# The first norm of a transformer layer on one core: block 1's row of scales read from PSUM, block 2's squares elsewhere, block 3's x turned

## The chip, the cores and the metric

The kernel runs on one core of a Trainium2 chip. Its engines work side by side, each through its own instructions in order: TensorE (PE; weight loads are shown as PEld), VectorE (DVE), ScalarE (ACT), GpSimd (POOL), and SyncE (SP), which here issues the DMAs. TensorE writes to PSUM alone; the other operands lie in SBUF. The metric is the time of one execution on the device, in microseconds (us); lower is better.

## The reference

One layer (DEPTH = 1, so the stick-breaking mixer) on 2048 tokens of 1024 features, 16 heads, followed by a SwiGLU FFN of width 2816. Cut to what matters:

```python
sh_m, sc_m, gt_m, sh_f, sc_f, gt_f = split(silu(c) @ ada_w + ada_b, 6)
h = rms_norm(x, norm_g[0]) * (1 + sc_m) + sh_m       # the first norm: the change is here
q, k, v = split(h @ w_qkv, 3)
z = q @ k.T * HEAD_DIM ** -0.5                       # per head, blocks of 128 rows
sp = where(s < t, softplus(z), 0)
a = exp(where(s < t, z - reverse_cumsum(sp), -inf))
x = x + gt_m * rms_norm((a @ v) @ w_o, norm_g[1])
h = rms_norm(x, norm_g[2]) * (1 + sc_f) + sh_f
g, u = split(h @ ffn_w_in, 2)
x = x + gt_f * rms_norm((silu(g) * u) @ ffn_w_out, norm_g[3])

rms_norm(x, g) = x * rsqrt(mean(x * x, -1) + 1e-6) * g
```

## The kernel before, in words

The 2048 tokens are four blocks of 512 (b = 0 to 3); the 1024 features are eight chunks of 128 (k = 0 to 7). The projections want h with features on the partitions, 128 x 512 for each block and chunk, and in two parts: a high part, which is h rounded to TensorE's fp32r type, and a low part, the rest. A product is then three matmuls (mm3, L174 to L176): high by high, high by low, low by high.

The first norm makes these parts (first_norm, L409, with modulate, L378). A block can get its transposed x in two ways. Blocks 0 and 2 load x by rows: the rows are squared and summed on ACT (rms_scale, L165), scaled by their rstd on DVE (L330, L338), turned on TensorE into PSUM (x_turn, L361), and then ACT multiplies by the gain and adds the shift (L383), and DVE rounds (L384) and subtracts (L385). Blocks 1 and 3, named in BY_FEATURES, load x a second time, by columns (cols_load, L313, the kernel argument xt). Of the rows only the rstd is used: spread over 128 columns (L340), it is turned on TensorE into a row of scales that is the same on all partitions (x_share, L352), and ACT copies it to SBUF (L354). scale_cols then multiplies a column chunk by gain and row on DVE (L372) or, for odd k of block 3, by the row alone on GpSimd (L376). modulate finishes: for even k and for all of block 1, ACT adds the shift and rounds (L389), DVE adds and subtracts (L390); for odd k of block 3, ACT applies gain and shift (L394), copies to the high part (L395) and GpSimd subtracts (L397). scale_cols runs up to two chunks ahead of modulate.

The program writes out the order of each engine's instructions by hand: what is traced first runs first on TensorE, ACT, DVE and GpSimd; SP's DMAs are placed by the framework. Buffers have tags with a number of slots; a new tile waits until a slot of its tag is free. Here matter "kt" (7: key tiles, columns of x), "v" (7: value tiles, rows of x), "wraw" (2: raw weights, junk of squares, the parked key and query tiles), "aT" (4: turned attention weights, and early on two weight tiles), "tmp" (4), and the PSUM pools zps (3 banks: scores), tps (2: turned weights) and accps (3: projections, turned values, the attention's sums, turned x).

project computes keys (t = 1), queries (t = 0), values (t = 2) of a pair of heads p and a block b, one mm3 per slice. While it runs for block b, the norm of the next block nb is made beside it: rows are squared and scaled at t = 0 (nb = 2) or t = 1 (nb = 3); chunks 0 to 2 of the norm at slices 2, 4, 6 of t = 2; chunks 3 to 7 at slices 0 to 4 of t = 1 in the next step, three products ahead of their use. Block 1's chunks 4 to 7 are made at the first slices of its own keys.

Attention runs at the same time, in slots of one 128 x 512 tile of scores. In a slot (ORDER_IN_SLOT) come, in order, the sum with values (L672), the scores (L593), one or two slices of the projections with what is beside them, the turning of weights (L644, every second slot), the two sigmoids on ACT (L610, L612), the scan on DVE (L622, L627) with a product on GpSimd (L634), and the turned weights' high part on ACT (L654) and low part on DVE (L660); in odd slots this last pair comes ahead of the sigmoids.

Of the kernel before, what the change touches and what calls it, by code (L numbers as in the profile page):

```python
# [16 lines left out]
P = 128  # L17
# [52 lines left out]

H2_STEP = 3

BY_FEATURES = (1, 3)

NORM_AT = [(2, 2), (2, 4), (2, 6)]

# [26 lines left out]
def hybrid_trunk_kernel(  # L103
# [206 lines left out]
    def cols_load(b, *which):  # L310
        for m in which or range(KC // 2):
            cols = att.tile([P, 2, BT], F32, name=f"xc{b}_{m}", tag="kt", bufs=BUFS["kt"])
            nc.sync.dma_start(cols, xt[b // 2, :, 2 * m : 2 * m + 2])  # L313
            x_cols[b, 2 * m], x_cols[b, 2 * m + 1] = cols[:, 0], cols[:, 1]

    def x_square(b, i):
        if b > 0:
            tok = x_tiles[b, i]
            if b in BY_FEATURES:
                junk = tok  # L320
            else:
                junk = att.tile([P, D], F32, name=f"xj{b}_{i}", tag="wraw", bufs=BUFS["wraw"])
            x_rstd[b, i] = rms_scale(att, tok, f"n0_{b}_{i}", junk=junk)
            return
        xn = att.tile([P, D], F32, name=f"xn{b}_{i}", tag="kt", bufs=BUFS["kt"])
        x_norm[b, i] = xn
        x_rstd[b, i] = rms_scale(att, x_tiles[b, i], f"n0_{b}_{i}", junk=xn)
# [16 lines left out]
    def x_share(b):  # L344

        if b not in BY_FEATURES:
            return
        pool, tag = (tps, "t") if b < 2 else (accps, "acc")
        pt = pool.tile([P, BT], F32, name=f"xr{b}", tag=tag)
        for i in range(4):  # L350
            tok = x_tiles.pop((b, i))
            nc.tensor.transpose(pt[:, i * P : (i + 1) * P], tok[:, :P], ident)  # L352
        x_row[b] = tok[:, BT:]
        nc.scalar.copy(x_row[b], pt)  # L354

    def x_turn(b, k):

# [8 lines left out]
    def scale_cols(b, k):  # L366

        if b not in BY_FEATURES:
            return
        u = x_cols[b, k]  # L370
        if k % 2 == 0 or b == 1:
            nc.vector.scalar_tensor_tensor(  # L372
                u, u, g_eff[:, 0, k : k + 1], x_row[b], op0=ALU.mult, op1=ALU.mult
            )
        else:
            nc.gpsimd.tensor_tensor(u, u, x_row[b], op=ALU.mult)  # L376

    def modulate(hl, b, k):  # L378

        gain, add = g_eff[:, 0, k : k + 1], mod[:, 0, k : k + 1]  # L380
        if b not in BY_FEATURES:
            u = att.tile([P, BT], F32, name=f"hf{b}_{k}", tag="tmp", bufs=BUFS["tmp"])
            nc.scalar.activation(u, x_turn(b, k), AF.Identity, bias=add, scale=gain)  # L383
            nc.vector.tensor_copy(hl[:, 0], u)  # L384
            nc.vector.tensor_tensor(hl[:, 1], u, f32(hl[:, 0]), op=ALU.subtract)  # L385
            return
        u = x_cols.pop((b, k))
        if k % 2 == 0 or b == 1:
            nc.scalar.activation(hl[:, 0], u, AF.Identity, bias=add)  # L389
            nc.vector.scalar_tensor_tensor(  # L390
                hl[:, 1], u, add, f32(hl[:, 0]), op0=ALU.add, op1=ALU.subtract
            )
        else:
            nc.scalar.activation(u, u, AF.Identity, bias=add, scale=gain)  # L394
            nc.scalar.copy(hl[:, 0], u)  # L395
            eng = nc.gpsimd if b == NB - 1 else nc.vector
            eng.tensor_tensor(hl[:, 1], u, f32(hl[:, 0]), op=ALU.subtract)  # L397

    def h_load(p, b):
        h = []  # L400
# [45 lines left out]
    def project(at):  # L446

        p, b = STEPS[at]
        begun = at < 2
        early, parked = (p, b) in EARLY, (p, b) == PARKED  # L450

        nb = STEPS[at + 1][1] if at + 1 < len(STEPS) and STEPS[at + 1][0] == 0 else None
        if STEPS[at] == (PARKED[0], 1):
            unpark()
        h = norm_h[b] if p == 0 or parked else h_load(p, b)

        def product(t):
            if begun:
                if at == 0 and t != 2:
                    first_norm(1, 2 + (t == 0))  # L460
                return first_acc[p, t]
            w = weights[p, t]
            acc = accps.tile([P, BT], F32, name=f"pj{p}_{b}_{t}", tag="acc")
            ahead = b == NB - 1 and p + 1 < NPAIR
            for k in range(KC):
                if t == 1:
                    if p == 0:
                        first_norm(b, k + (4 if b == 1 else 3))
                    if k == 0 and nb == 3:
                        cols_load(3)  # L470
                    if k in (3, 5) and waiting:
                        waiting.pop(0)()
                if nb == 2 and (t, k) == (0, 0):
                    x_load(3)
                square_at = {2: 0, 3: 1}.get(nb)
                if t == square_at and k < 4:
                    x_square(nb, k)
                if t == square_at and 2 <= k < 6:
                    x_spread(nb, k - 2)
                if nb and (t, k) == (0, 1):  # L480
                    x_share(nb)
                if (t, k) in NORM_AT:
                    first_norm(nb, NORM_AT.index((t, k)))
                if ahead and k == 0:
                    load_weights(p + 1, t)
                if ahead and k == 6:
                    split_weights(p + 1, t)
                mm3(acc, (w[0][:, k], w[1][:, k]), (h[k][:, 0], h[k][:, 1]), k == 0, k == KC - 1)
                yield
            return acc  # L490

        def split(acc, tag):
            place = "wraw" if parked else "qkn"
            hl = att.tile([P, 2, BT], F32R, name=f"{tag}n{p}_{b}", tag=place, bufs=BUFS[place])
            nc.scalar.copy(hl[:, 0], acc)
            nc.vector.tensor_tensor(hl[:, 1], acc, f32(hl[:, 0]), op=ALU.subtract)
            return hl

        closing = (p, b) == (NPAIR - 1, NB - 1)
        if closing:  # L500
            wo_load(0, 0, "whl")
            wo_load(0, 1, "ht")
        n = split((yield from product(1)), "k")
        if closing:
            wo_load(0, 2, "whl")
        if parked:
            nc.sync.dma_start(k_park, f32(n))
        else:
            kt = att.tile([P, 2, BT], F32R, name=f"kt{p}_{b}", tag="kt", bufs=BUFS["kt"])
            for e in range(2):  # L510
                for part in range(2):
                    nc.sync.dma_start(
                        f32(kt[part * HD : (part + 1) * HD, e]), f32(n[e * HD : (e + 1) * HD, part])
                    )
            keys[p, b] = kt

        n = split((yield from product(0)), "q")
        if closing:
            wo_load(0, 3, "whl")
        if parked:  # L520
            nc.sync.dma_start(q_park, f32(n))
            for out_of in held:
                nc.sync.dma_start(*out_of)
        else:
            qt = att.tile([P, 2, 2, BT], F32R, name=f"qt{p}_{b}", tag="qt", bufs=BUFS["qt"])
            for e in range(2):
                for half in range(2):
                    nc.sync.dma_start(
                        f32(qt[half * HD : (half + 1) * HD, e]), f32(n[e * HD : (e + 1) * HD])
                    )  # L530
            queries[p, b] = qt
        acc = yield from product(2)
        tag = "w" if early else "tmp"
        vT = att.tile([P, BT], F32, name=f"vT{p}_{b}", tag=tag, bufs=BUFS[tag])
        nc.scalar.copy(vT, acc)

        def values_turn():
            pool, ptag = (zps, "z") if early else (accps, "acc")
            pt = pool.tile([P, 4, 2, HD], F32, name=f"vt{p}_{b}", tag=ptag)
            for i in range(4):  # L540
                nc.tensor.transpose(
                    pt[:, i].rearrange("p e d -> p (e d)"), vT[:, i * P : (i + 1) * P], ident
                )
            v = att.tile([P, 4, 2, 2, HD], F32R, name=f"v{p}_{b}", tag="v", bufs=BUFS["v"])
            nc.scalar.copy(v[:, :, :, 0], pt)
            nc.vector.tensor_tensor(v[:, :, :, 1], pt, f32(v[:, :, :, 0]), op=ALU.subtract)
            if parked:
                nc.sync.dma_start(v_park, f32(v))
            else:
                values[p, b] = v  # L550

        if early:
            waiting.append(values_turn)
            return
        for _ in range(VGAP):
            yield
        values_turn()
# [1200 lines left out]
```

## Time and profile before

| what | us |
|---|---|
| three runs: median (lowest to highest) | 2848.71 (2847.3 to 2853.94) |
| the profiled execution | 2845.32 |
| its span, first to last instruction | 2843.2 |
| TensorE busy in the span | 2800.4 (98%) |
| VectorE busy | 2021.7 (71%) |
| ScalarE busy | 1634.1 (57%) |
| GpSimd busy | 1282.5 (45%) |
| mean granted TensorE clock | 0.997 |

A row of the timeline reads: start in us, length in us, engine, line of the kernel, operation, out<-in by the program's names, shapes, how many were merged, and in brackets the idle time of the engine just before and what ended it. A row of a group (by line) ends in busy us and the mean ns of one; a row asked by tile or line gives the shortest, the median and the longest in ns, and the first and last start in us. A row of the waits gives the total in us, the number of times and the longest. A DMA row gives the KB of one and the us from issue to landing. Starts are counted from the start of the span.

### The profile page before, as it was taken

The page shows a single profiled execution, that of the slowest core. Times are in us where ns is not written, and L with a number is a line of the kernel's source. Part 1 is how long each engine was busy: PE and PEld are TensorE (multiplying, and loading weights), DVE is VectorE, ACT ScalarE, POOL GpSimd, SP SyncE. Part 2 cuts the span into 40 slices and gives each one's busy share as a digit, 9 for nine tenths or more (in the row PEclk, how much of TensorE's full clock was granted, in tenths as well). Part 3 has the DMA queues.
Part 4 walks back from the last instruction along what each step waited for, and adds up shares of the span by engine and source line. Part 5 has one row for each costly group of instructions (what it writes and reads, how often), then busy time and mean ns, then how long its engine had stood idle before and what let it go on. Part 6 is the DMA issues. An engine that isn't in the chain of part 4 may idle for free.

```text
span 2843.2 us, 41829 instructions
## 1 busy us (share of the span) xinstructions
PE 2800.4 (98%) x13853; PEld 2338.5 (82%) x13853; DVE 2021.7 (71%) x2822; ACT 1634.1 (57%) x3274; POOL 1282.5 (45%) x2032
## 2 busy tenths in 40 slices
PE   9899999999999999999999999999999999999998
PEld 7788888888888888887888788888788888888887
DVE  6788888888888888888866766555775655134377
ACT  5787778787777877778645533333433333322243
POOL 0565666676576655666410122222222222544454
PEclk9999999999999999999999999999999999999999
DMA  9774556666665635546389644334453335545575
GB/s 368 285 230 157 186 170 212 211 188 216 196 217 177 218 116 175 193 136 228 97 293 317 196 139 153 120 103 160 127 176 110 112 105 166 191 138 153 181 227 187
DMA packets 239787, 521.05 MB, mean 183 GB/s; under 512 B 22481, under 2 KB 108497, under 8 KB 222674
## 3 DMA queue, kind: packets, MB, share of 16 engines
q1 hardware_dynamic: 239570, 518.38, 56.4%
q8 instruction: 109, 1.79, 0.3%
q14 instruction: 108, 0.88, 0.1%
HBM read 351.04 MB, written 118.49 MB: 165 GB/s over the span
## 4 chain that ended last, share of the span: by engine, by line
PE 84%; DVE 5%; DMA 5%; ACT 2%; issue 2%; POOL 1%; SPq 0%; DVEq 0%; POOLq 0%; ACTq 0%
PE s L174 9%; PE s L175 9%; PE s L176 9%; PE z L593 8%; PE o L672 8%; PE t L644 8%; PE pj L174 5%; PE pj L176 5%; PE pj L175 5%; PE o L176 4%; PE o L174 4%; PE o L175 4%; DMA h_s<-ht 1%; PE y L176 1%; PE y L174 1%
## 5 line engine op out<-in xcount | busy, mean ns | idle before, releaser
L634 POOL TENSOR_TENSOR a<-a,w 128x512 f32<-128x512 f32 (+3 forms) x640 | 621.6, 971 | 217.2 <-DVE w L627 130.3
L627 DVE TENSOR_TENSOR_SCAN w<-z,c,begin 128x512 f32<-128x512 f32 x384 | 489.3, 1278 | 83.9 <-ACT z L612 60.6
L174 PE MATMUL s<-r,l 128*128 128x512 f32 x1232 | 482.3, 391 | 5.1 <-DVE p L1490 3.9
L176 PE MATMUL s<-r,l 128*128 128x512 f32 x1232 | 480.2, 390 | 0.0
L175 PE MATMUL s<-r,l 128*128 128x512 f32 x1232 | 479.9, 390 | 0.0
L610 ACT ACTIVATE a<-z 128x512 f32<-128x512 f32 (+3 forms) x640 | 347.1, 542 | 170.4 <-PE z L593 137.6
L672 PE MATMUL o<-aT,v 128*128 128x512 f32 (+3 forms) x1280 | 385.0, 382 | 0.1
L660 DVE TENSOR_TENSOR aT<-t,aT 128x512 fp32r<-128x512 f32 (+3 forms) x640 | 358.6, 594 | 23.9 <-ACT aT L654 23.4
L593 PE MATMUL z<-kt,qt 128*128 128x512 f32 (+3 forms) x1280 | 363.7, 365 | 0.0
L654 ACT CAST aT<-t 128x512 fp32r<-128x512 f32 (+3 forms) x640 | 313.9, 533 | 73.5 <-PE t L644 63.4
L612 ACT ACTIVATE z<-z 128x512 f32<-128x512 f32 (+3 forms) x640 | 344.8, 539 | 0.0
L1498 POOL TENSOR_TENSOR one<-p,p 128x512 f32<-128x512 f32 x44 | 70.9, 1612 | 579.1 <-issue 322.2
L174 PE MATMUL pj<-ht,w 128*128 128x512 f32 x768 | 308.4, 402 | 4.3 <-issue 1.4
L644 PE MATMUL t<-begin,a 128*128 128x128 f32 x2176 | 295.7, 274 | 13.8 <-DVE aT L660 12.5
L644 PEld LDWEIGHTS t<-begin,a 128*128 128x128 f32 x2176 | 255.7, 141 | 64.1 <-DVE aT L660 14.0
L175 PE MATMUL pj<-ht,w 128*128 128x512 f32 x768 | 301.5, 393 | 2.0 <-DVE ht L390 1.5
L176 PE MATMUL pj<-ht,w 128*128 128x512 f32 x768 | 301.9, 393 | 0.0
L174 PEld LDWEIGHTS s<-r,l 128*128 128x128 f32 x1232 | 231.7, 188 | 56.0 <-ACT l L1351 2.9
L176 PEld LDWEIGHTS s<-r,l 128*128 128x128 f32 x1232 | 231.5, 188 | 48.3
L175 PEld LDWEIGHTS s<-r,l 128*128 128x128 f32 x1232 | 231.7, 188 | 48.0 <-issue 0.5
L622 DVE TENSOR_TENSOR_SCAN w<-z,begin 128x128 f32<-128x128 f32 (+3 forms) x256 | 208.6, 817 | 76.7 <-ACT z L612 67.5
L593 PEld LDWEIGHTS z<-kt,qt 128*128 128x128 f32 x1280 | 231.0, 189 | 37.6 <-DVE w L622 0.2
(178 smaller groups left out, 4879.3 us busy)
## 6 DMA issues: line engine op xcount, KB each, us to landing
ht<-h_s SPq DMA_DIRECT2D x108, 1024.0 KB, 8.2
wi<-in_win SPq DMA_DIRECT2D x86, 512.0 KB, 4.0
qt<-qn SPq DMA_DIRECT2D x124, 256.0 KB, 4.8
ol_qt<-act_s SPq DMA_DIRECT2D x56, 512.0 KB, 3.7
act_s<-S SPq DMA_DIRECT2D x66, 256.0 KB, 4.1
br<-in_wout SPq DMA_DIRECT2D x66, 256.0 KB, 3.5
h_s<-ht SPq DMA_DIRECT2D x16, 1024.0 KB, 9.8
o_s<-os SPq DMA_DIRECT2D x128, 128.0 KB, 2.6
```

Of the source, the lines that this page charges most:

```text
L174: nc.tensor.matmul(acc, lhs[0], rhs[0], start=first, stop=False, **kw)
L175: nc.tensor.matmul(acc, lhs[0], rhs[1], start=False, stop=False, **kw)
L176: nc.tensor.matmul(acc, lhs[1], rhs[0], start=False, stop=last, **kw)
L593: nc.tensor.matmul(z[:, :n], q[:, e, part, r * P : (r + 1) * P], k[:, e, :n], start=part == 0, stop=part == 1,)
L610: nc.scalar.activation(a[:, :n], z[:, :n], AF.Sigmoid, scale=QK_SCALE)
L612: nc.scalar.activation(z[:, :n], z[:, :n], AF.Sigmoid, scale=-QK_SCALE)
L627: nc.vector.tensor_tensor_scan(rest[:, rev], left[:, rev], begin[:, :BT][:, rev], initial=carries[r], op0=ALU.mult, op1=ALU.bypass,)
L634: nc.gpsimd.tensor_tensor(a[:, :n], a[:, :n], rest[:, 1 : n + 1], op=ALU.mult)
L644: nc.tensor.transpose(pt[:, rb * P : (rb + 1) * P], weighed[i, rb][:, j * P : (j + 1) * P], ident)
L654: nc.scalar.copy(hl[:, 0, t0:], pt[:, t0:])
L660: nc.vector.tensor_tensor(hl[:, 1, t0:], pt[:, t0:], f32(hl[:, 0, t0:]), op=ALU.subtract)
L672: nc.tensor.matmul(acc[:, t0:], lhs, hl[:, part, t0:], start=sc == qb and j == 0 and part == 0, stop=sc == 0 and j == 3 and part == 1,)
```

## The change

Block 1 stays by columns. Its row of scales is no longer copied to SBUF: DVE reads it from the PSUM bank in each of the eight chunks. For k = 3, 5 and 7 ACT adds the shift in place, copies to the high part, and GpSimd makes the low part. Block 2's squares write their junk to "aT" instead of "wraw". Block 3 leaves BY_FEATURES: it no longer loads columns, scales its whole rows on DVE, has its x turned on TensorE into an accps bank, and DVE applies gain and shift straight from PSUM to a "tmp" tile; ACT copies that to the high part and GpSimd subtracts, for all eight chunks. Its junk of squares goes to "wraw". The argument xt now holds block 1 alone.

```diff
-BY_FEATURES = (1, 3)
+BY_FEATURES = (1,)
+
+ON_GPSIMD = (3, 5, 7)
...
-            nc.sync.dma_start(cols, xt[b // 2, :, 2 * m : 2 * m + 2])
+            nc.sync.dma_start(cols, xt[:, 2 * m : 2 * m + 2])
...
-                junk = att.tile([P, D], F32, name=f"xj{b}_{i}", tag="wraw", bufs=BUFS["wraw"])
+                place = "aT" if b == 2 else "wraw"
+                junk = att.tile([P, D], F32, name=f"xj{b}_{i}", tag=place, bufs=BUFS[place])
...
-        pool, tag = (tps, "t") if b < 2 else (accps, "acc")
-        pt = pool.tile([P, BT], F32, name=f"xr{b}", tag=tag)
+        pt = tps.tile([P, BT], F32, name=f"xr{b}", tag="t")
...
-        x_row[b] = tok[:, BT:]
-        nc.scalar.copy(x_row[b], pt)
+        x_row[b] = pt
...
-        if k % 2 == 0 or b == 1:
-            nc.vector.scalar_tensor_tensor(
-                u, u, g_eff[:, 0, k : k + 1], x_row[b], op0=ALU.mult, op1=ALU.mult
-            )
-        else:
-            nc.gpsimd.tensor_tensor(u, u, x_row[b], op=ALU.mult)
+        nc.vector.scalar_tensor_tensor(
+            u, u, g_eff[:, 0, k : k + 1], x_row[b], op0=ALU.mult, op1=ALU.mult
+        )
...
             u = att.tile([P, BT], F32, name=f"hf{b}_{k}", tag="tmp", bufs=BUFS["tmp"])
+            if b == NB - 1:
+                nc.vector.tensor_scalar(u, x_turn(b, k), gain, add, op0=ALU.mult, op1=ALU.add)
+                nc.scalar.copy(hl[:, 0], u)
+                nc.gpsimd.tensor_tensor(hl[:, 1], u, f32(hl[:, 0]), op=ALU.subtract)
+                return
...
-        if k % 2 == 0 or b == 1:
-            nc.scalar.activation(hl[:, 0], u, AF.Identity, bias=add)
-            nc.vector.scalar_tensor_tensor(
-                hl[:, 1], u, add, f32(hl[:, 0]), op0=ALU.add, op1=ALU.subtract
-            )
-        else:
-            nc.scalar.activation(u, u, AF.Identity, bias=add, scale=gain)
+        if k in ON_GPSIMD:
+            nc.scalar.activation(u, u, AF.Identity, bias=add)
             nc.scalar.copy(hl[:, 0], u)
-            eng = nc.gpsimd if b == NB - 1 else nc.vector
-            eng.tensor_tensor(hl[:, 1], u, f32(hl[:, 0]), op=ALU.subtract)
+            nc.gpsimd.tensor_tensor(hl[:, 1], u, f32(hl[:, 0]), op=ALU.subtract)
+            return
+        nc.scalar.activation(hl[:, 0], u, AF.Identity, bias=add)
+        nc.vector.scalar_tensor_tensor(
+            hl[:, 1], u, add, f32(hl[:, 0]), op0=ALU.add, op1=ALU.subtract
+        )
...
-                    if k == 0 and nb == 3:
-                        cols_load(3)
...
-        "xt": get("x")[0].reshape(NB, BT, KC, P).transpose(0, 3, 2, 1)[1::2],
+        "xt": get("x")[0].reshape(NB, BT, KC, P).transpose(0, 3, 2, 1)[1],
```

## The prediction

> **What bounds the kernel now.** The span on the page comes first, then the busy time by stretch, because the change touches only the first norm, which is over at about 145 us.
>
> ```profile
> span 2843.2 us, 41829 instructions
> ...
> 55.00:70.00 15.00, 13.47 (x64) 10.64 (x63) 13.91 (x22) 9.89 (x17) 0.00 (x0) 1.00 0.93 296
> 70.00:84.00 14.00, 12.46 (x53) 9.84 (x52) 6.90 (x15) 7.33 (x14) 3.25 (x5) 0.88 1.01 408
> 84.00:98.00 14.00, 12.99 (x69) 9.61 (x68) 11.52 (x24) 12.25 (x26) 6.18 (x13) 0.99 0.97 355
> 98.00:112.00 14.00, 14.00 (x79) 11.98 (x78) 10.21 (x19) 9.52 (x24) 5.52 (x17) 1.00 1.00 344
> 112.00:130.00 18.00, 13.97 (x73) 11.86 (x72) 15.48 (x20) 12.58 (x29) 14.82 (x23) 0.91 0.61 191
> 130.00:145.00 15.00, 12.63 (x62) 8.99 (x61) 11.31 (x14) 13.69 (x26) 12.31 (x15) 1.00 0.52 193
> 145.00:1500.00 1355.00, 1341.02 (x7308) 1133.96 (x7308) 1142.69 (x1535) 1034.66 (x2188) 809.71 (x1674) 1.00 0.59 191
> ```
>
> The columns are the stretch, its length, the busy time of TensorE (PE), its weight loads, VectorE (DVE), ScalarE (ACT) and GpSimd (POOL), the granted TensorE clock, the DMA share and GB/s. From 145 us on TensorE is busy 99% of the time, so a microsecond won or lost ahead of that is kept to the end. What can be won is TensorE's idle time between 55 and 145 us: 1.53 + 1.54 + 1.01 + 0 + 4.03 + 2.37 = 10.5 us, and the lowered clock: (1 - 0.88) x 14 = 1.7 and (1 - 0.91) x 18 = 1.6 us. The whole of it is 13.8 us, 0.48% of the span. DMA is full until 112 us. The waits of TensorE in that part name the owners:
>
> ```profile
> PE t L644 <- DVE aT L660: 6.0, 4, 2.3
> PE xT L361 <- DVE x L338: 1.5, 3, 0.7
> PE pj L175 <- DVE ht L390: 1.5, 1, 1.5
> ```
>
> The first is block 3's (the attention's turned weights, whose low parts come late from DVE), the second block 2's, the third block 1's.
>
> **Block 1: the row of scales read from PSUM, three lows on GpSimd.**
>
> ```profile
> 55.47 0.59 ACT L354 COPY x<-xr 128x512 f32<-128x512 f32 x1 [2.01 <-PE xr L352]
> ...
> 56.09 2.08 DVE L372 SCALAR_TENSOR_TENSOR xc<-xc,g_eff,x 128x512 f32<-128x512 f32 x3 [1.43 <-ACT x L354]
> ...
> 66.57 0.49 PE L175 MATMUL pj<-ht,w 128*128 128x512 f32 x1 [1.53 <-DVE ht L390]
> ...
> L390 DVE SCALAR_TENSOR_TENSOR ht<-xc,mod,ht x12: 739/745/1373, 58.1 to 137.4; 128x512 fp32r<-128x512 f32 x12
> ...
> L395 ACT CAST ht<-xc x4: 618/620/622, 117.8 to 140.7; 128x512 fp32r<-128x512 f32 x4
> L397 POOL TENSOR_TENSOR ht<-xc,ht x4: 1258/1280/1296, 121.2 to 142.3; 128x512 fp32r<-128x512 f32 x4
> ```
>
> The ACT copy goes, so DVE starts its scalings 0.6 us sooner. The low part of column 3 leaves DVE ahead of the one that TensorE waits for (column 4), another 0.75: the wait of 1.53 shrinks to about 0.2. ACT pays 3 x 0.62 for the copies and saves 0.59; GpSimd does 3 x 1.28 in a stretch where it has nothing (0.00). The last of these, column 7, comes one ACT copy and one GpSimd pass after its column, so some 0.7 us of wait can return there. Net at 70 us: -0.7 (bounds -1.5 and +0.3).
>
> **Block 2: squares in other buffers.** The four squares now wait for a parked key tile to leave its buffer.
>
> ```profile
> 72.68 1.06 ACT L165 ACTIVATE xj<-x 128x1024 f32<-128x1024 f32 x1 [2.00 <-DMA k_park<-kn]
> ...
> 82.33 2.45 SPq L307 DMA_DIRECT2D x<-in_x  x1
> ...
> x<-in_x SPq DMA_DIRECT2D x1, 512.0 KB, 6.8
> ...
> 89.57 1.05 ACT L165 ACTIVATE x<-x 128x1024 f32<-128x1024 f32 x1
> ...
> 91.61 0.77 ACT L383 ACTIVATE hf<-xT,mod,g_eff 128x512 f32<-128x512 f32 x1
> ```
>
> Without that wait the squares start 2.0 + 0.7 us sooner, the waits of 1.5 us on the scaled x go, and with them the lowered clock (1.7). TensorE would be about 4 us ahead at 84 us. But ACT is in order, and between block 2's columns 3 and 4 stands the first square of block 3 (the row at 89.57). Its x is issued at 82.33 and takes 6.8 us: it lands at 89.1, 0.4 us ahead of its use. The change takes no byte from the queue ahead of that load, and DMA is full; only the 0.6 us by which the first keys leave sooner passes on. So ACT stands until 88.5, and the next column (91.61) comes 1.0 us sooner, not 4. TensorE then stands idle there instead, for some 3 us, and I charge that what the idle in 70 to 84 us and its 1.7 us of clock showed, less the 1.0 us of idle that 84 to 98 us has to take it up: +0.7. Net at 98 us: -0.3; bounds -4.4 (no such gate) and +0.7 (nothing passed on).
>
> By the Trainium skill, TensorE: Matmul & The Clock Gate, What's actually happening, the clock falls after an idle window of about 3.4 us and is binary. Here it fell with 1.54 us of idle in 14, spread over short waits, so the trace is harsher than that sentence; by the page alone the 0.7 would not be charged and the sum would be 0.7 us lower.
>
> **Block 3's x in rows instead of columns.**
>
> ```profile
> L338 DVE TENSOR_SCALAR x<-x,n_rstd x4: 741/744/753, 76.2 to 78.7; 128x1024 f32<-128x1024 f32 x4
> ...
> 95.94 0.28 DVE L340 TENSOR_SCALAR x<-ones,n_rstd 128x128 f32<-128x128 f32 x1
> ...
> 84.69 0.60 PE L361 MATMUL xT<-begin,x 128*128 128x128 f32 x4
> ...
> 113.63 0.73 ACT L389 ACTIVATE ht<-xc,mod 128x512 fp32r<-128x512 f32 x1 [1.49 <-DVE xc L372]
> ...
> 121.25 1.79 DVE L372 SCALAR_TENSOR_TENSOR xc<-xc,g_eff,x 128x512 f32<-128x512 f32 x1
> ...
> 121.24 1.26 POOL L397 TENSOR_TENSOR ht<-xc,ht 128x512 fp32r<-128x512 f32 x1
> ...
> L998 DVE COPY yh<-y 128x512 f32<-128x512 f32 x4 | 2.7, 672 | 0.5 <-ACT y_junk L978 0.5
> ```
>
> Scaling whole rows costs DVE 4 x (0.74 - 0.28) = 1.8 us at 95 to 101 us; one of the four stands ahead of block 2's column 6, for which TensorE waits on DVE already: +0.5 (0 to +1.8). The four transposes of the row of scales go: -0.35. The 2 MB of columns are no longer loaded; nothing on the path waited for them, and SP and DMA only get room: 0 (down to -0.5).
>
> Per column block 3 now needs four transposes on TensorE (about 0.35 us from start to the next matmul, as at 84.69), one DVE pass from PSUM (0.67, the nearest row with one PSUM source), one ACT copy (0.62) and one GpSimd subtraction (1.28). Before, the eight columns took four DVE pairs (0.75 + 0.75 and more), four ACT passes of 0.73 and four pairs on ACT, and four GpSimd pairs. By totals this relieves DVE and ACT. By order it does not. Each slot of attention has on ACT: the norm's copy, two sigmoids; on DVE: the norm's pass, the scan. Before, ACT's norm input was made one to two columns ahead. Now ACT's copy waits for a DVE pass of the same slot, which stands behind the scan of the slot before, which waits for ACT's sigmoids of that slot. DVE and ACT take turns. The row at 113.63 shows one such turn: ACT idle for 1.49 us.
>
> ```profile
> 128.98 0.60 PE L541 MATMUL vt<-begin,vT 128*128 128x128 f32 x4
> ...
> 134.32 0.39 PE L174 MATMUL pj<-ht,w 128*128 128x512 f32 x1
> ...
> 135.01 0.39 PE L174 MATMUL pj<-ht,w 128*128 128x512 f32 x1
> ...
> 130.23 0.69 DVE L546 TENSOR_TENSOR v<-vt,v 128x512 fp32r<-128x512 f32 x1 [1.11 <-ACT v L545]
> ...
> 133.56 0.59 ACT L610 ACTIVATE a<-z 128x512 f32<-128x512 f32 x1
> 134.04 0.60 ACT L612 ACTIVATE z<-z 128x512 f32<-128x512 f32 x1
> ...
> 135.59 1.28 DVE L627 TENSOR_TENSOR_SCAN w<-z,c,begin 128x512 f32<-128x512 f32 x1
> ...
> 144.29 0.79 PE L644 MATMUL t<-begin,a 128*128 128x128 f32 x3
> ```
>
> One turn: 0.67 + 0.62 + 0.59 + 0.60 + 1.28, and one half of the turned weights (about 0.6) in between: 4.3 us, less 0.3 for handovers that overlap by 0.1 (133.56 + 0.59 is past 134.04): 4.0. TensorE's own pace is 2.9: from 128.98 to 144.29 it ran six slots with their waits, 2.55 each, and 0.35 of transposes comes on top. Columns 3 to 7 fall in four slots in a row, two of them (the projection's third and fourth products, 134.32 and 135.01) in one, which adds one more pass and copy (1.3). Column 3 also needs a third accumulator bank while values are turned (128.98) and the attention's sum is open: it waits until 130.92, then transposes, ready at 131.6. 131.6 + 4 x 4.0 + 1.3 = 148.9, where the turned weights that wait for the last of it now begin at 144.29: +4.6. Covers: GpSimd's lows run beside this, three products ahead of their use. Bounds: -2.4 (all idle of 130 to 145 us gone) and +8 (the same, with two lowered windows of 1.7).
>
> Columns 0 to 2 fall in slots with others between, so a turn is partly made good: DVE drops the slow pass of 1.79 us but gains a wait for ACT. +0.4, between -4.0 (the idle of 112 to 130 us gone) and +3.3 (three turns of 1.1 over TensorE's pace).
>
> By the Trainium skill, SBUF — State Buffer, Who interferes with whom, a DVE instruction with two SBUF inputs and a GpSimd instruction that reads SBUF block each other, and one with a PSUM input does not. The rows at 121.25 and 121.24 agree (1.79 us instead of 0.75, beside a GpSimd pass); by that rule block 3 sheds about 2.2 us of such excess, and if DVE's totals decided, the sum would be some 7 us lower. That is the first rival.
>
> **Sum.** -0.3 + 0.5 - 0.35 + 0 + 0.4 + 4.6 = +4.85 us. The profiled execution took 2845.3 us (2.1 beside its span); the sum gives 2850.2. The median of three runs is 2848.7, 3.4 above that execution, so as a median: 2853.5.
>
> **Rivals.** (A) DVE and ACT do not fall into step: the idle of 112 to 145 us (6.4) and its clock (1.6) go, eight groups of transposes cost 2.8, the rest -0.15: -5.4 us, median 2843.3. For it: DVE's load falls, the slow passes go. Against: ACT idle at 113.63, the same order. (A') Besides, x of block 3 lands sooner and the idle of 55 to 84 us with its clock goes (3.1 + 1.7), in place of the -0.3: -9.9, median 2838.8, faster. Against: DMA share 1.01 there. (B) Slower: the turn-taking holds in all eight columns' slots, three more at 1.1 = 3.3, less the 0.4 charged, and two windows fall to half clock (3.3): +11.0, median 2859.7. It decides (over +8.5) once seven of eight columns cost a full turn and one window falls. For it: idle of 4.03 us in 112 to 130 lowered the clock already. Against: slots between columns 0, 1 and 2. (C) The transposes only fill old idle time, and the accumulator wait of 1.6 us (129.3 to 130.9) alone is added to -0.15: +1.4, median 2850.1.
>
> **Numbers.** Less than 0.3% (8.5 us) is about what a measurement of this kernel can tell from no change. Forecast 0.50, C 0.08, A 0.12 (all three within), A' 0.07 (faster), B 0.23 (slower). Range 2842 to 2861: from A to B.
>
> **What would show it.** Right: no ACT wait on the parked keys, but one on block 3's first x at about 85 to 88.5 us, and the next column's ACT pass near 90.6; in 128 to 150 us DVE passes on xT directly behind scans, ACT copies idle before them, TensorE waiting on aT. Wrong: block 2's columns 4 us sooner at 92 us; TensorE without gaps in 112 to 145; a wait for an accumulator bank elsewhere.

## The result and the profile after

The changed kernel took 2856.55 us (median; 2851.76 to 2865.37), the kernel before, on the same chips, 2850.53 (2844.52 to 2856.76), each of 22 runs. The ratio is 1.0022 [1.0014, 1.0031]: 6.0 us slower by the medians. The interval leaves out 1, but the step is less than the 0.3% that the prediction counts as no change. The forecast was 2853.5 and +4.85.

The profiled executions stand 15.8 us apart, and most of that is not the change. Stretches of the kernel after, from the span's start, with the columns as in the prediction:

```profile
span 2859.0 us, 41891 instructions
...
16.00:24.00 8.00, 8.00 (x38) 7.79 (x38) 2.22 (x4) 1.96 (x3) 0.05 (x1) 1.00 1.03 410
24.00:32.00 8.00, 7.98 (x33) 7.21 (x32) 4.79 (x5) 6.59 (x9) 0.00 (x0) 1.00 1.03 409
32.00:42.00 10.00, 10.00 (x35) 8.53 (x34) 6.64 (x12) 2.18 (x4) 0.00 (x0) 1.00 1.03 415
...
98.00:112.00 14.00, 10.02 (x46) 7.51 (x45) 10.62 (x20) 11.81 (x25) 6.56 (x11) 0.88 1.00 363
...
130.00:145.00 15.00, 11.09 (x60) 9.04 (x59) 9.17 (x15) 9.78 (x23) 8.65 (x17) 0.89 0.51 159
```

The first three of these stretches in the kernel before:

```profile
16.00:24.00 8.00, 7.98 (x58) 7.58 (x59) 4.05 (x6) 5.12 (x7) 0.22 (x1) 0.79 1.03 411
24.00:32.00 8.00, 8.00 (x48) 6.93 (x48) 7.14 (x10) 4.90 (x7) 0.00 (x0) 1.00 1.03 408
32.00:42.00 10.00, 10.00 (x50) 8.32 (x48) 9.86 (x22) 4.21 (x6) 0.00 (x0) 1.00 1.03 415
```

From 16 to 42 us TensorE is busy without a pause in both, yet it does 106 matmuls after and 156 before. It runs the same instructions at about half speed for longer (rows are in the last section), and nothing of the change has run yet. I call the time up to the changed code the lead-in; the two kernels must be laid on each other behind it. I take the start of the 140th projection matmul (counted from 0), the last point ahead of the changed code, and compare starts of the same matmuls from there. The first and the last such row, of the kernel before and of the kernel after:

```profile
60.53 0.39 PE L176 MATMUL pj<-ht,w 128*128 128x512 f32 x1
145.63 0.40 PE L174 MATMUL pj<-ht,w 128*128 128x512 f32 x1
```

```profile
70.83 0.39 PE L178 MATMUL pj<-ht,w 128*128 128x512 f32 x1
162.88 0.40 PE L176 MATMUL pj<-ht,w 128*128 128x512 f32 x1
```

The lead-in differs by 70.83 - 60.53 = 10.3 us; the change costs (162.88 - 70.83) - (145.63 - 60.53) = +6.95 us. It stands within 0.1 us of that through the attention (to 1388 us of before), and +5.5 is left at the end of the span (what took back the other 1.5 us behind the attention isn't known). A table of such differences to the kernel before, for every run told of below, in us; the columns are the times in the kernel before (block 1 done, block 2's squares done, block 2's column 4 past, attention's first sum with values, columns 0 to 2 of block 3 past, the norm over), and the second is the lead-in's difference, which is left out of the others. Each row is one execution; line numbers in the rows shown below shift by a few from kernel to kernel.

| run | lead-in | 69 | 82 | 98 | 104 | 124 | 146 |
|---|---|---|---|---|---|---|---|
| after | 10.3 | -0.7 | -3.5 | -0.2 | +0.7 | +1.8 | +7.0 |
| e5_again: the same kernel | 5.9 | -0.7 | -3.5 | -1.0 | 0.0 | +1.0 | +5.8 |
| e1_blocks12: blocks 1 and 2 alone | 2.6 | -0.7 | -3.5 | +0.2 | +0.6 | +0.5 | +0.5 |
| e2_block3: block 3 alone | 10.3 | 0.0 | -0.7 | +0.4 | +1.4 | +2.3 | +7.2 |
| e3_ahead | 3.3 | -0.7 | -3.5 | -0.7 | +0.3 | -1.6 | -3.0 |
| e9_late | 2.8 | -0.7 | -3.5 | -0.7 | +0.3 | +1.3 | +2.0 |
| e10_soon | 6.8 | -0.7 | -3.5 | -0.2 | +0.8 | -1.9 | +3.1 |
| e8_b3ahead | 0.3 | 0.0 | +0.4 | +0.6 | +1.5 | -0.5 | -1.8 |
| e6_onact | 10.5 | -0.7 | -3.5 | -0.8 | +0.1 | -2.3 | -2.2 |
| e4_early | -0.1 | -0.7 | -3.5 | -4.0 | +4.0 | +5.0 | +11.9 |
| e7_hold | 5.5 | -0.7 | -3.5 | -4.0 | +3.2 | +1.5 | +0.1 |

Where the 7 us lie is told by the waits of the kernel after up to 165 us, first of TensorE, then of ACT (us in total, times, longest):

```profile
PE t L644 <- DVE aT L660: 5.0, 6, 2.0
PE xT L362 <- ACT hf L386: 3.7, 1, 3.7
PE xT L362 <- DVE hf L382: 3.2, 2, 3.0
PE pj L176 <- DVE v L546: 1.0, 1, 1.0
PE pj L177 <- POOL ht L394: 0.6, 1, 0.6
```

```profile
ACT ht L383 <- DVE hf L382: 14.9, 8, 2.4
ACT xj L167 <- DMA x<-in_x: 3.7, 1, 3.7
```

The old waits of block 2 on its scaled x are gone. In their place stand one wait of 3.7 us on block 2's ACT pass, at whose root ACT stands 3.7 us for block 3's first x, and 3.2 us on block 3's scaled chunks. ACT's copy of all eight chunks stands for DVE, 1.9 us each. The waits on late turned weights, which a lighter DVE might have removed, are still there: 5.0 us, after 6.0.

### The profile page after: what moved, and what is told of

It reads as the page before. It is cut to its first block, busy times and chain, and to the rows that moved or that the text cites. A ratio compares the mean times of both kernels' runs of the same rounds, so it can differ in the third digit from the quotient of the medians.

```text
span 2859.0 us, 41891 instructions
## 1 busy us (share of the span) xinstructions
PE 2813.1 (98%) x13881; PEld 2349.7 (82%) x13881; DVE 2017.9 (71%) x2819; ACT 1631.9 (57%) x3271; POOL 1285.2 (45%) x2035
## 3 DMA queue, kind: packets, MB, share of 16 engines
q8 instruction: 109, 1.79, 0.3%
## 4 chain that ended last, share of the span: by engine, by line
PE 84%; DVE 4%; issue 3%; ACT 2%; POOL 1%; DMA 1%; SPq 0%; DVEq 0%; POOLq 0%; ACTq 0%
PE s L176 9%; PE s L177 9%; PE s L178 9%; PE o L672 8%; PE z L593 8%; PE t L644 8%; PE pj L176 5%; PE pj L178 5%; PE pj L177 5%; PE o L178 4%; PE o L177 4%; PE o L176 4%; PE y L178 2%; PE y L176 2%; PE y L177 2%
```

## The experiments

**Each half of the change alone, and both halves with one thing moved.** Four kernels ran beside each other and the kernel before (2851.6 us, 28 runs).

Blocks 1 and 2 changed, block 3 as before (e1_blocks12; by columns, its passes as they were; the main lines, against the kernel after):

```diff
-BY_FEATURES = (1,)
+BY_FEATURES = (1, 3)
...
+        if b == 3 and k % 2 == 1:
+            nc.scalar.activation(u, u, AF.Identity, bias=add, scale=gain)
...
```

> The changed kernel with block 3 as before (by columns, its old scaling and modulation); the changes to blocks 1 and 2 stay. If the loss is in block 3 (turn-taking of DVE and ACT, the reading of the prediction), it is gone: between 1 us shorter and 1 us longer than the kernel before. In the trace block 2's squares start without a wait, and ACT still stands some 3 us ahead of the first square of block 3, since its x lands no sooner. Rival: if blocks 1 and 2 are to blame (three more ACT copies, GpSimd's lows, a row read from PSUM), it stays 3 to 6 us longer than before.

Measured: 2851.12 us, ratio 0.9996 [0.9985, 1.0007]. The 3.5 us won by 82 us are handed back by 98 us, and +0.5 is left at the end of the norm. ACT stands 3.4 us for block 3's first x here too, and TensorE 3.5 us for the ACT pass behind it. So blocks 1 and 2 alone move nothing, and the gate belongs to them, not to block 3's new way.

Block 3 by rows in the kernel before, blocks 1 and 2 untouched (e2_block3):

```diff
-BY_FEATURES = (1, 3)
+BY_FEATURES = (1,)
...
+            if b == NB - 1:
+                nc.vector.tensor_scalar(u, x_turn(b, k), gain, add, op0=ALU.mult, op1=ALU.add)
+                nc.scalar.copy(hl[:, 0], u)
+                nc.gpsimd.tensor_tensor(hl[:, 1], u, f32(hl[:, 0]), op=ALU.subtract)
+                return
```

> The kernel before with block 3's change alone (x turned, gain and shift from PSUM on DVE, copy on ACT, subtraction on GpSimd). Turn-taking: 5 to 7 us longer than before, with ACT's copies waiting about 2 us each for DVE's pass in the slots of columns 3 to 7, and TensorE's turned weights late. Rival (the parts need each other): under 2 us longer.

Measured: 2857.21 us, ratio 1.0019 [1.0008, 1.0030], and +7.2 us in the table. Its waits:

```profile
ACT ht L385 <- DVE hf L384: 14.9, 8, 2.4
```

```profile
PE xT L361 <- DVE hf L384: 3.2, 2, 3.0
```

These two sums are those of the kernel after, to a tenth. What the change costs lies in block 3, but for the 0.5 us above.

The kernel after, with block 3's transposes and DVE pass made one column ahead of ACT's copy (e3_ahead, main lines); no operation is added or dropped:

```diff
...
             if b == NB - 1:
-                nc.vector.tensor_scalar(u, x_turn(b, k), gain, add, op0=ALU.mult, op1=ALU.add)
+                for n in range(0 if k == 0 else k + 1, min(k + 2, KC)):
+                    u = att.tile([P, BT], F32, name=f"hf{b}_{n}", tag="tmp", bufs=BUFS["tmp"])
+                    nc.vector.tensor_scalar(u, x_turn(b, n), ...)
+                    x_cols[b, n] = u
+                u = x_cols.pop((b, k))
                 nc.scalar.copy(hl[:, 0], u)
```

> The changed kernel with one edit: block 3's transposes and its DVE pass are made one column ahead of ACT's copy. The work is the same, instruction for instruction. Turn-taking: ACT no longer waits for a pass of its own slot, so most of the 5.2 us of the stretch between the turning of block 2's values and the end of block 3's norm comes back: 3 to 5 us shorter than the changed kernel, about 1 us longer to 2 us shorter than the kernel before. Rival (the eight groups of transposes on TensorE are the price, 2.8 us): no more than 1 us comes back.

Measured: 2844.45 us, ratio 0.9984 [0.9974, 0.9994]: faster than both kernels. The expectation had the direction and not the size: 3 to 5 us shorter than the kernel after were expected, and it is 10 us by the table and 12 by the medians, since it counted columns 3 to 7 alone. In the table it goes from +0.3 at 104 us to -3.0, where the kernel after goes from +0.7 to +7.0. ACT's wait and TensorE's on late turned weights:

```profile
ACT ht L389 <- DVE hf L383: 3.4, 3, 1.6
```

```profile
PE t L651 <- DVE aT L667: 0.6, 1, 0.6
```

With the same transposes, the same DVE passes and the same GpSimd passes, 14.9 us of ACT's waiting become 3.4, and 5.0 us of TensorE's become 0.6. So the price of block 3 is neither the transposes nor the work given to an engine, but that DVE's pass and ACT's copy of one column stand in the same slot. The two engines then form a ring: the pass, the copy, the sigmoids, the scan and the next pass, each behind the one before. (From 146 us to the end this execution drew 4.0 us further ahead of the kernel before. One part of it is a lowered clock at 2010 us that it happened not to have; the rest I can't name. The norm is worth 3.0 us.)

The kernel after, with block 3's x loaded as soon as block 2's rows are out of their buffers (e4_early):

```diff
-                if nb == 2 and (t, k) == (0, 0):
+                if nb == 2 and (t, k) == (1, 0):
                     x_load(3)
```

> The changed kernel with one edit: block 3's rows of x are asked for about 8 product slices sooner, ahead of the second block's keys. If ACT's wait ahead of the first square of block 3 is the gate that takes back block 2's gain, this wait of 3.7 us in the trace goes, and the half clock after it: 2.5 to 4.5 us shorter than the changed kernel, 2 to 4 us longer than the kernel before. Rival (ACT would be late there anyway, or the keys that now come later are missed by TensorE): under 1 us.

Measured: 2857.78 us, ratio 1.0025 [1.0014, 1.0036]. The gate is gone: at 98 us the kernel is 4.0 us ahead, where the kernel after is 0.2. But 2.5 to 4.5 us shorter than the kernel after were expected, and that missed: at 104 us it is 4.0 us behind the kernel before, and at the end of the norm 11.9, where the kernel after has 7.0.

```profile
102.93 0.66 PE L593 MATMUL z<-kt,qt 128*128 128x128 f32 x2 [6.05 <-DMA qt<-qn]
103.39 0.73 PE L176 MATMUL pj<-ht,w 128*128 128x512 f32 x1
103.92 0.63 PE L177 MATMUL pj<-ht,w 128*128 128x512 f32 x1
104.35 0.63 PE L178 MATMUL pj<-ht,w 128*128 128x512 f32 x1
```

```profile
85.66 2.82 SPq L426 DMA_DIRECT2D h_s<-ht  x2
90.62 6.16 SPq L528 DMA_DIRECT2D qt<-qn  x4
```

The attention's first scores wait 6.05 us for their query tiles, and the matmuls behind the wait take 0.63 us instead of 0.39: half clock (0.50 granted from 103 to 106.5 us). The first of those tiles landed 10.9 us after its issue, where in the kernel before it took 5.0. With the lead-ins taken off it was issued 3.9 us sooner and landed 2.0 us later: what moved forward pushes the tiles back. Two of the four stores of block 2's norm (h_s, 1 MB each) stand right ahead of them at the queue.

**Again, and with DVE out of the ring.** Four kernels beside the kernel before (2850.06 us, 29 runs). The kernel after once more, for the lead-in (e5_again):

> The changed kernel once more, one execution with a profile. The profiles so far differ by up to 10 us between the first instruction and the 140th projection matmul, in kernels whose instructions there are the same. If that is TensorE's clock at the start of an execution, and not the change, this execution may have another lead-in than the 10.3 us (over the kernel before) of the first profile of this kernel, and from that matmul to the end of the first norm it is again 6.9 us behind the kernel before, within 0.5. Rival: the lead-in is the change's own; it is 10.3 again.

Measured: 2856.53 us. Its lead-in is 5.9 us longer than that of before, where the first profile's was 10.3, with the same instructions. Behind it the two agree within 0.9 us up to 124 us and stand at +5.8 and +7.0 at the end of the norm, 1.1 us apart, where within 0.5 was expected. So a difference of 1 us between two rows of the table is not yet one between two kernels.

Block 3's gain and shift on ACT instead of DVE (e6_onact):

```diff
-                nc.vector.tensor_scalar(u, x_turn(b, k), gain, add, op0=ALU.mult, op1=ALU.add)
+                nc.scalar.activation(u, x_turn(b, k), AF.Identity, bias=add, scale=gain)
                 nc.scalar.copy(hl[:, 0], u)
```

> The changed kernel with block 3's gain and shift on ACT (one pass from PSUM with both, as for block 2) in place of DVE; the copy on ACT and the subtraction on GpSimd stay, as do the transposes. ACT gets 0.78 us more for each column, DVE loses 0.79. Turn-taking between DVE and ACT: the norm's chain no longer passes through DVE, 3 to 7 us shorter than the changed kernel. Rival (ACT is what is short: it gets 8 x 0.78 = 6.2 us more work): as long as the changed kernel, or up to 4 us longer.

Measured: 2849.29 us, ratio 0.9990 [0.9980, 1.0001], -2.2 us in the table. ACT does eight passes more than in the kernel after, and by the table it is 8 to 9 us faster, more than the 3 to 7 that were expected; by the measured times it can't be told from the kernel before. Both passes of a column now stand on one engine, and ACT's waits of 14.9 us for DVE's pass are gone. Of TensorE's 5.0 us on late turned weights this is left:

```profile
PE t L644 <- DVE aT L660: 1.1, 2, 0.6
```

One column ahead, x loaded early as above, and block 2's four stores of h held until its columns are made (e7_hold; the main lines of the last of its three edits):

```diff
-            if b == 1 and k < 4:
+            if b == 1 and k < 4 or b == 2:
                 held.append(out_of)
...
+                    while k == 5 and b == 2 and p == 0 and held:
+                        nc.sync.dma_start(*held.pop(0))
...
```

> Block 3's pass one column ahead (as in the experiment with that edit alone), its rows of x asked for sooner, and the four stores of block 2's norm held back until its eight columns are made, behind the query tile of the second block. If the gate at 89 to 103 us is the order of bytes in a full DMA queue, the wait on x goes and the query tile is no longer late, since 4 MB now stand behind it: 3 to 4.5 us shorter than with the pass one column ahead alone, 6 to 8 us shorter than the kernel before. Rival (what is held back is missed later, or DMA is full for other reasons): 0 to 3 us longer than with the pass ahead alone.

Measured: 2848.38 us, ratio 0.9996 [0.9984, 1.0008]. This missed: the wait for the query tiles is still 5.0 us, and with it +3.2 at 104 us. But the trace shows that the hold did not come about:

```profile
91.12 2.79 SPq L479 DMA_DIRECT2D h_s<-ht  x2
96.04 5.64 SPq L537 DMA_DIRECT2D qt<-qn  x4
```

Two of the four held stores are still issued ahead of the query tiles, at the same place as in e4_early (the lead-ins differ by 5.6 us). So this run repeats the early load, now with the pass one column ahead, and does not test whether the tiles stand behind those stores. From 84 to 112 us its DMA share is 1.01 still; which bytes would have to go is open.

Block 3 by rows and one column ahead, with blocks 1 and 2 as before (e8_b3ahead; the main lines, against the kernel before):

```diff
-BY_FEATURES = (1, 3)
+BY_FEATURES = (1,)
...
+            if b == NB - 1:
+                for n in range(0 if k == 0 else k + 1, min(k + 2, KC)):
...
```

> Block 3 by rows with its pass one column ahead, blocks 1 and 2 as in the kernel before. If what blocks 1 and 2 gain is handed back at block 3's x, this is as short as with their changes: 2 to 4 us shorter than the kernel before. Rival (their changes carry part of the gain): 0 to 1 us shorter than the kernel before.

Measured: 2849.31 us, ratio 0.9994 [0.9983, 1.0004], -1.8 us in the table beside -3.0 with blocks 1 and 2 changed (e3_ahead). That lies between the two forecasts. By the traces blocks 1 and 2 carry 1.2 us of that lead, hardly more than two executions of one kernel differ by, and by the measured times the two intervals overlap.

**Where the turn-taking costs.** The one-column lead only from column 3 on (e9_late), and only up to column 2 (e10_soon), beside the kernel before (2851.34 us, 19 runs). The edits are shown against e3_ahead. In both, column 3 itself is still made in its own slot:

```diff
-                for n in range(0 if k == 0 else k + 1, min(k + 2, KC)):
+                for n in range(k if k < 4 else k + 1, min(k + (k > 2) + 1, KC)):
```

> The changed kernel, with block 3's transposes and DVE pass made one column ahead of ACT's copy only from column 3 on; columns 0 to 2 stay in step as in the changed kernel. Prediction's split (0.4 us in columns 0 to 2, 4.6 in columns 3 to 7): counted from the 140th projection matmul, the end of the norm stands at about -2.5 us against the kernel before, hardly other than with all columns ahead (-3.0), and ACT's waits on block 3's scaled chunks shrink to under 6 us. Rival (a third or more of the price lies in columns 0 to 2, whose slots also take full turns): +0.5 to +1.5 us there, with a wait of TensorE on the late low part of the turned weights left between columns 0 and 2.

```diff
-                for n in range(0 if k == 0 else k + 1, min(k + 2, KC)):
+                for n in range(k if k in (0, 3, 4, 5, 6, 7) else k + 1, min(k + (k < 2) + 1, KC)):
```

> The changed kernel, with block 3's transposes and DVE pass made one column ahead only in columns 0 to 2; columns 3 to 7 stay in step. Prediction's split: the end of the norm hardly better than in the changed kernel, +5.5 to +6.5 us against before. Rival (a third or more of the price lies in columns 0 to 2): +2.5 to +3.5 us. In both, the wait of about 3 us before column 4's transposes stays.

Measured: 2849.21 us, 1.0004 [0.9989, 1.0018], and 2851.36 us, 0.9999 [0.9988, 1.0009]. By the measured times neither can be told from the kernel before. In the table the first ends at +2.0 and the second at +3.1: the rival's side, though the first lies 0.5 us above its range, and ACT still waits 9.5 us in it, where under 6 were expected. From 104 to 124 us and from 124 to 146 us the kernels gain or lose:

| | columns 0 to 2 | columns 3 to 7 |
|---|---|---|
| in step (after) | +1.0 | +5.2 |
| in step from column 3 on (e10_soon) | -2.7 | +5.0 |
| in step up to column 2 (e9_late) | +1.0 | +0.7 |
| nowhere in step (e3_ahead) | -2.0 | -1.4 |

Rows that differ in one part alone give its price. Columns 0 to 2 in step cost 3.0 us (e9_late less e3_ahead) to 3.7 (after less e10_soon), columns 3 to 7 cost 4.5 (after less e9_late, where column 3 is still in step) to 6.4 (e10_soon less e3_ahead). Most of the spread in the latter is the lowered clock: between the last two columns of the table the granted clock is 0.94 in the kernel after, in e9_late and in e10_soon, which makes 1.3 to 1.6 us, and 1.00 in e3_ahead. In e9_late it falls behind the waits of columns 0 to 2. The expectation took the prediction's 0.4 for that price, which is wrong: 0.4 was the difference to the kernel before, which has 4.03 us of idle there itself. Measured so, columns 0 to 2 are at +1.0. In the kernel without the ring from column 3 on, TensorE's waits are these:

```profile
125.80 0.44 PE L651 MATMUL t<-begin,a 128*128 128x128 f32 x2 [0.97 <-DVE aT L667]
128.23 0.45 PE L651 MATMUL t<-begin,a 128*128 128x128 f32 x1 [1.99 <-DVE aT L667]
134.70 0.66 PE L362 MATMUL xT<-begin,x 128*128 128x128 f32 x4 [0.96 <-DVE v L553]
...
142.05 0.66 PE L362 MATMUL xT<-begin,x 128*128 128x128 f32 x4 [0.92 <-DVE hf L383]
```

The first two are the turned weights behind columns 0 to 2 (0.95 and 2.00 in the kernel after), the third is the accumulator bank, here at column 4's transposes. The kernel after has a wait of 2.96 us before the transposes of column 6 (by their order; the expectations above call them column 4's). Here it is gone, and 0.92 stands before column 7's. In the kernel without the ring up to column 2, of the first two one of 0.95 is left, on GpSimd's product, and these stay, the second of them before column 6's transposes:

```profile
135.59 0.50 PE L176 MATMUL pj<-ht,w 128*128 128x512 f32 x1 [0.96 <-DVE v L553]
...
144.76 0.66 PE L362 MATMUL xT<-begin,x 128*128 128x128 f32 x4 [2.96 <-DVE hf L383]
```

## Why the prediction was right

The sign, the place and the mechanism were right; the size was 1.2 us short against the measured times, 2.1 against the first profile and 1.0 against the second. Of the 2.1, spreading and transposes are 0.8, columns 0 to 2 and columns 3 to 7 are 0.6 each, and what came before is 0.1.

**Block 1, -0.7.** Measured -0.67. The wait of about 0.7 us that was to return at column 7 is there, on GpSimd's low part (0.6 in the waits above). No wait of TensorE names the copies on ACT.

**Block 2, -0.3 net at 98 us.** Measured -0.23, and -0.98 the second time. The step as forecast, in the kernel after:

```profile
80.26 1.06 ACT L167 ACTIVATE xj<-x 128x1024 f32<-128x1024 f32 x1
...
99.17 1.06 ACT L167 ACTIVATE xj<-x 128x1024 f32<-128x1024 f32 x1 [3.66 <-DMA x<-in_x]
...
101.22 0.76 ACT L386 ACTIVATE hf<-xT,mod,g_eff 128x512 f32<-128x512 f32 x1
...
102.03 0.66 PE L362 MATMUL xT<-begin,x 128*128 128x128 f32 x4 [3.75 <-ACT hf L386]
```

Block 2's first square waits for nothing any more. Block 3's first square is ready 3.66 us before its x. Less the lead-in of 10.29, it starts at 88.9, and the next column's pass at 90.9, where the forecast had 88.5 and near 90.6. The gap of 3.75 us on TensorE was forecast as some 3. The run with the earlier load shows that this gate held the 4 us: without it they are there at 98 us. The reason given, that the load gains little in a full queue, fits: with the lead-in taken off, x was issued 1.1 us sooner than in the kernel before (81.2 instead of 82.3) and landed 0.3 us sooner (88.9 instead of 89.1). That run, and e7_hold, add that an earlier load only finds the next gate, so A' could not have come about by the load alone.

By the Trainium skill, TensorE: Matmul & The Clock Gate, What's actually happening, an idle window of about 3.4 us lowers the clock. This wait agrees (3.75 us, and 0.88 as the granted clock of that stretch). The stretch of 130 to 145 us doesn't: its clock is 0.89, and its longest wait is 2.00 us.

**Spreading on DVE, +0.5, and the transposes gone, -0.35.** From 98 to 104 us the kernel after loses 0.97 us and the second profile the same, where +0.15 was forecast. But the kernel with blocks 1 and 2 alone loses 0.4 there too and block 3 alone 1.0, so not all of it is the row scaling; the prediction's own upper end, +1.8 - 0.35, holds it.

**Columns 0 to 2, +0.4.** Measured +1.0, in both profiles and once more in the kernel that is in step only there. "A turn is partly made good" was right in kind. But the turn-taking is there in full: by e9_late and e10_soon it costs 3.0 to 3.7 us, and +1.0 is what is left of it since a kernel that is not in step there gains 2.0 to 2.7 us on the kernel before. So the small net term was partly luck. Two of the turned weights still wait 1.0 and 2.0 us, the waits that this lighter DVE would have been free to remove.

**Columns 3 to 7, +4.6.** Measured +5.2, and +4.9 in the second profile and in the run of block 3 alone. One turn in the kernel after:

```profile
147.04 0.78 DVE L382 TENSOR_SCALAR hf<-xT,g_eff,mod 128x512 f32<-128x512 f32 x1
...
147.86 0.62 ACT L383 CAST ht<-hf 128x512 fp32r<-128x512 f32 x1 [2.05 <-DVE hf L382]
...
148.38 0.59 ACT L610 ACTIVATE a<-z 128x512 f32<-128x512 f32 x1
...
148.87 0.59 ACT L612 ACTIVATE z<-z 128x512 f32<-128x512 f32 x1
149.39 0.59 ACT L654 CAST aT<-t 128x512 fp32r<-128x512 f32 x1
149.55 1.28 DVE L627 TENSOR_TENSOR_SCAN w<-z,c,begin 128x512 f32<-128x512 f32 x1 [1.73 <-issue]
...
150.75 0.67 DVE L660 TENSOR_TENSOR aT<-t,aT 128x512 fp32r<-128x512 f32 x1
...
151.34 0.80 DVE L382 TENSOR_SCALAR hf<-xT,g_eff,mod 128x512 f32<-128x512 f32 x1
152.17 0.62 ACT L383 CAST ht<-hf 128x512 fp32r<-128x512 f32 x1 [2.19 <-DVE hf L382]
152.19 0.65 PE L362 MATMUL xT<-begin,x 128*128 128x128 f32 x4 [2.96 <-DVE hf L382]
```

From one pass to the next: 151.34 - 147.04 = 4.30 us, where 4.0 was forecast. In the chain the pass, the copy, the two sigmoids, the scan, the low part of the turned weights and the next pass follow each other: each begins as the one before it ends, on the other engine or its own. DVE stands 1.73 us before the scan and ACT 2.19 before the copy, in the same slot. The pass takes 0.78 to 0.81 us, where I took 0.67 from another line. The other two turns take 4.16 and 4.24 us, and the slot with two columns adds 1.54, where 1.3 was forecast. TensorE stands 2.96 us before column 6's transposes, since the bank that they are to fill is read by that pass, column 5's. The wait for an accumulator bank is 1.0 instead of 1.6, so the longer turns and the shorter wait offset each other in part. It stands at the projection's first product and not at column 3's transposes. A wait for such a bank elsewhere was one of the prediction's signs of being wrong; here it took the place of the one that was forecast.

**The rivals.** A stood on DVE's totals. Over the same work, here columns 0 to 2 and then columns 3 to 7, these are the kernel before and the kernel after (of the busy times in a row, the third is DVE's and the fourth ACT's):

```profile
103.86:124.32 20.46, 16.43 (x90) 13.59 (x88) 15.85 (x22) 14.29 (x31) 13.99 (x22) 1.00 0.82 277
124.32:145.63 21.31, 18.94 (x92) 14.78 (x92) 15.96 (x21) 17.07 (x33) 16.62 (x27) 0.92 0.52 189
```

```profile
114.89:136.37 21.48, 18.12 (x102) 14.78 (x100) 13.21 (x20) 11.66 (x25) 12.15 (x22) 1.00 0.55 157
136.37:162.88 26.51, 21.06 (x112) 16.62 (x112) 17.69 (x23) 16.35 (x36) 15.17 (x27) 0.94 0.56 200
```

DVE falls from 31.8 to 30.9 us in all, ACT from 31.4 to 28.0, and no pass of block 3 takes 1.79 us. By the Trainium skill, SBUF — State Buffer, Who interferes with whom, a DVE instruction with at most one SBUF input, outside the modes that use both ports, doesn't contend with GpSimd; the eight passes, which read x from PSUM, agree (0.784 to 0.812 us, with GpSimd busy beside them). The relief was real, though small for DVE, and lay off the path: the ring handed it back. Only with the ring opened does the time come to A's side (e3_ahead, 7.2 us under the kernel before by the medians and 4.6 by the ratio; A gave 5.4). (The prediction gave two prices for A, some 7 us under its sum by the rule on DVE and GpSimd and 10.2 in the list of rivals; the second is the one that its median goes by.) B had the mechanism of columns 0 to 2 nearer than the forecast: its 3.3 is what the turn-taking costs there. But against the kernel before they cost 1.0, and the clock, lowered in the norm's last part before (0.92) as after (0.94), adds nothing. C is out, by the price of block 3 alone.

## What to carry to other kernels

In this kernel, engines in order that hand a tile to each other within one slot take turns, however little each has to do. So before moving a pass to a less loaded engine, follow one slot around all of them and add up the ring, and if it is longer than the slot, make the first pass one step ahead of the second (here worth 9 to 10 us by the table, with no operation added). With the DMA queue full, a gain ahead of a load's landing was handed back here at that load, and moving the load forward showed the next one. Whether a change in the order of DMAs came about is to be seen in the trace before its result is read: one of the two here did not. And before two profiles are compared by stage, lay them on each other at the last instruction that both share unchanged.

## What the runs showed of the hardware

TensorE's lead-in differs between executions of the same instructions. In the kernel after, projection matmuls up to 41 us take 0.63 us each and from then on 0.39, though no idle time stands between them:

```profile
31.85 3.41 PE L708 MATMUL acol<-c_act,ar 128*128 128x1 f32 x16
...
40.38 0.63 PE L176 MATMUL pj<-ht,w 128*128 128x512 f32 x1
...
41.22 0.39 PE L178 MATMUL pj<-ht,w 128*128 128x512 f32 x1
```

In the second profile of the same kernel that point comes at 31.5 us. In the kernel before the clock is full from 22.7 us on. The lead-ins of the eleven profiles in the table lie between 0.1 us less and 10.5 us more than that of before, and the same kernel has 10.3 and 5.9. That is about the size of the 12 to 14 us between the lowest and the highest time of one kernel, and the two profiled executions of the kernel after, 4.4 us apart in the lead-in, took 2861.2 and 2856.5 us. Among the early matmuls are rows of sixteen with a single column to move, such as the one shown (3.41 us); whether these keep the clock low wasn't tried. The granted clock of the stretches doesn't show it (1.00 in 32 to 42 us): the durations of the matmuls do.

By the Trainium skill, TensorE: Matmul & The Clock Gate, What's actually happening, the ramp takes a run-variable time of less than 1% of a kernel's span. The traces agree on both (10.5 of 2850 us is 0.4%); for a change of 0.2% it is still larger than what is looked for.
